# Products of 512 columns whose moving operand is read from its two halves in turn

## The chip, the core and the metric

The kernel runs on one core of a Trainium2 chip. The metric is the device time of one execution in microseconds (us), lower is better; the median of three runs stands for a kernel. The engines are named as in the profile: PE is TensorE with its matrix products, PEld its loads of stationary operands, DVE is VectorE, ACT ScalarE, POOL GpSimd, SP SyncE, whose queue issues most DMA transfers. Operands lie in SBUF, results of products in PSUM, in banks of 512 float32 columns on 128 partitions.

## What is computed

The reference is float32 throughout: two layers of a first block, then two layers of a second one, on 512 tokens of width 1024 (and, in the second, 256 tokens of context). Shortened to the products that matter:

```python
def swiglu(u, w_in, w_out):                     # w_in [1024, 2*2816], w_out [2816, 1024]
    gate, up = jnp.split(u @ w_in, 2, axis=-1)
    return (jax.nn.silu(gate) * up) @ w_out

# first block, layer l: FFN, mixer, FFN, each with residual, layer norm and modulation
f = swiglu(modulate(x, sh1, sc1), ffn_in[l, 0], ffn_out[l, 0])
x = deepnorm_residual(x, f, g1, ln_g[l, 0], ln_b[l, 0], 0.5)
u = modulate(x, sh2, sc2)
m = even_mixer(u, ...) if l % 2 == 0 else odd_mixer(u, ...)   # RG-LRU and linear attention / MLA
x = deepnorm_residual(x, m, g2, ln_g[l, 1], ln_b[l, 1])
f = swiglu(modulate(x, sh3, sc3), ffn_in[l, 1], ffn_out[l, 1])
x = deepnorm_residual(x, f, g3, ln_g[l, 2], ln_b[l, 2], 0.5)

# second block, layer l: one wide projection, three branches, their gated sum
h = rms_norm(x, norm_g[l]) * (1 + scale) + shift
(a_glu, a_gate, nq, nk, nv, n_gate, wq, wk, wv, w_gate, merge) = split(h @ w_in[l])  # [1024, 7936]
y = sig(g_a) * conv_branch(...) + sig(g_b) * neighbourhood(...) + sig(g_c) * window(...)
x = x + gate * (y @ w_o[l])
```

## The kernel before

[...] Each operand x is split into a part `hi`, rounded to float32r, and `lo = x - hi` (`split`, L118 on ACT and L119 on DVE; weights in `wsplit`, L129 and L130), and a product is hi·hi + hi·lo + lo·hi into one bank of PSUM. `mm3` (L148 to L153) writes this for a stationary weight block w of 128x128 and a moving operand x of up to 512 token columns:

```python
mm(out, lhsT=w[0], rhs=x[0], start=first, stop=False)   # L151
mm(out, lhsT=w[0], rhs=x[1], start=False, stop=False)   # L152
mm(out, lhsT=w[1], rhs=x[0], start=False, stop=last)    # L153
```

`lhsT` is the stationary operand, `rhs` the moving one. There are four families of products with 512 moving columns:

- Feature-major, `feat` and `ffn_first` through `mm3` (L151 to L153): the moving operand is the transposed activations `xTh`, `xTl` [128, 8, 512], eight k tiles for one bank. FFN inputs, the projections of the mixers and the MLA queries and keys are made so. With the first column pair of an FFN and a few others the tokens come in two slices of 256.
- Token-major, `tok_out.go` (L322, L323, L326): the outputs of FFNs and mixers. Stationary is a slice of 128 tokens of the activations (`gh`, `gl`), moving are 512 columns of the weights (`whi`, `wlo`), into eight banks for four token tiles and two halves of the 1024 columns.
- `proj_steps` (L1071, L1072, L1076): the wide projection of the second block, feature-major, and beside it products of 256 context columns (L1074, L1075, L1078).
- `out_proj.go` (L1851, L1852, L1855): the last projection of a layer of the second block, token-major.

Beside these stand products of 256 columns and fewer (attention scores, transposes, L1127 to L1129 token-major) and the plain float32 products of RG-LRU (L568).

What comes out of a bank is read by ACT or DVE: `gated` of the FFN by ACT (silu, L407) and DVE (product, L408), `resid_ln` by DVE (L285, then layer norm), the mixers by ACT (L613 to L716), the second block by ACT (L1605, L1649 to L1688, L1823) and DVE (L1616, L1618, L1651, L1653), the last result by DVE (L2299, followed by the output DMA).

The order of the work is that of the code: each engine has its own list, and units that follow one another by some ticks (`tick`, `push`) are emitted between products. Weights come through `raw` (L121), two buffers of 1 MB filled by SP's queue, and are split a unit ahead of their products. Modulation vectors for later layers are computed in the background (`bg_step`) on DVE from `gv` tiles.

Of the kernel before, what the change touches and what calls it, by code (L numbers as in the profile page):

```python
# [32 lines left out]

class Core:
# [98 lines left out]
    def wcols(self, w, c0, n=256, lows=None):  # L133
        """w [K, N] columns c0..c0+n as one unit; (hi, lo) [P, K/P, 128] per block."""
# [4 lines left out]
    def wrows(self, w, r0, a=2, gate=None, eng=None):  # L139
        """w [K, 1024] rows r0.. as one unit; (hi, lo) [P, 1, 1024] per k tile, columns times gate, on eng[j]."""  # L140
# [7 lines left out]
    def mm3(self, out, w, x, first, last):  # L148
        """out += w.T @ x, both in two parts; w stationary."""
# [20 lines left out]
    def rstd_fast(self, v, n, eps, scale):  # L170
        """the same, by a square root and a Newton step."""
# [26 lines left out]
    def load_cols(self, out, parts):  # L198
        """background steps: DRAM rows of 128 as the columns of out [P, rows]."""
# [6 lines left out]
    def gemv(self, w, accs):  # L206
        """accs: list of (acc tile [P, 1024], columns [P, 8]); one step per unit."""
# [17 lines left out]
    def col_fold(self, acc, tmp):  # L225
        """first half of the sum of acc [P, 1024 or 512] over the partitions; tmp like acc."""
# [6 lines left out]
    def col_fin(self, r, bcol, out):  # L233
        """second half, as columns, plus bcol."""
# [8 lines left out]
    def row_out(self, col, out):  # L243
        """columns [P, 8] to a row of DRAM."""
# [32 lines left out]
    def resid_ln(self, t, ps2):  # L277
        """x of token tile t, normalised."""
# [13 lines left out]
    def affine_rows(self, xs, g, b, scale, row, eng):  # L292
        """background steps: x*g*scale + b*scale for the tiles xs; g, b [1024] in DRAM, row: a tile for them."""
# [64 lines left out]
    def ffn_first(self, pool, g, w_in, weights, gated, first):  # L358
        """the first four column blocks of both parts; the operands come by halves of the k tiles,
# [2021 lines left out]
```

## Time and profile before

| | us |
|---|---|
| median of three runs (3640.43 to 3645.78) | 3644.38 |
| span of the profiled execution | 3646.3 |
| PE busy in it | 3522.6 |
| DVE busy | 2459.3 |
| ACT busy | 1446.6 |
| POOL busy | 654.7 |

A busy time is the time in which an engine has an instruction under way. Matrix products overlap in the records: one of 512 columns is shown as 0.39 to 0.40 us long, and the next begins 0.23 us after it. The distance between starts, or the length of a gapless window over its count of products, is thus what one costs. A line in the profile carries the line number of the code; a group "L151 PE MATMUL ps<-xTh,whi 128\*128 128x512" has the moving operand first, then the stationary one, the stationary shape, and the result's shape. A few per cent of the product records can be missing.

### The profile page before, as it was taken

To read this page: it belongs to the slowest core of one execution; us is meant where nothing else is said; L and a number is where in the kernel's file an instruction comes from. 1 tells how busy PE (TensorE), PEld (TensorE's weight loads), DVE (VectorE), ACT (ScalarE), POOL (GpSimd) and SP (SyncE) were. 2 spreads that over 40 slices of the span, in tenths; PEclk is the share of its full clock that TensorE was granted. 3 is DMA by queue.
4 is the path that set the end of the run, shared out by engine and by line. 5 is a ranking of instruction groups with operands and counts; after the bars stand their busy time and mean duration, and the time that the engine had idled before them with its cause. 6 is when DMAs were issued, how large, how long until landed. Compare 5 with 4: busy or idle time off the path is not lost. (4 is left out here: it accounts for less than half of the span.)

```text
span 3646.3 us, 49117 instructions
## 1 busy us (share of the span) xinstructions
PE 3522.6 (97%) x19303; PEld 2970.0 (81%) x19303; DVE 2459.3 (67%) x3978; ACT 1446.6 (40%) x2576; POOL 654.7 (18%) x734
## 2 busy tenths in 40 slices
PE   8999999999999999989999999989999999979999
PEld 6788887788878888878888898878888888868887
DVE  7665545866665785586886577797774467796854
ACT  3222344643223222364322265545323255546342
POOL 1200211000000000041000124696000133390001
PEclk9999999999999999999999999999999999999999
DMA  7762322236742663222663232211112243211233
GB/s 261 240 212 93 100 76 81 87 108 192 237 144 93 223 198 104 69 69 70 207 221 116 93 102 59 60 35 30 53 59 81 76 147 93 56 51 36 87 99 110
DMA packets 264739, 412.82 MB, mean 113 GB/s; under 512 B 16385, under 2 KB 209658, under 8 KB 264378
## 3 DMA queue, kind: packets, MB, share of 16 engines
q1 hardware_dynamic: 251274, 380.33, 32.1%
q0 software_dynamic: 9040, 23.31, 2.6%
q10 hardware_dynamic: 4192, 6.03, 0.5%
q8 instruction: 152, 2.49, 0.3%
q14 instruction: 81, 0.66, 0.1%
HBM read 395.45 MB, written 10.39 MB: 111 GB/s over the span
## 5 line engine op out<-in xcount | busy, mean ns | idle before, releaser
L129 ACT ACTIVATE whi<-raw 128x1024 fp32r<-128x1024 f32 (+2 forms) x532 | 538.2, 1015 | 1175.1 <-PE ps L152 470.1
L130 DVE TENSOR_TENSOR wlo<-raw,whi 128x1024 fp32r<-128x1024 f32 (+2 forms) x530 | 644.0, 1217 | 337.8 <-ACT whi L129 336.0
L151 PE MATMUL ps<-xTh,whi 128*128 128x512 f32 (+2 forms) x1971 | 737.5, 375 | 4.6 <-ACT xTh L118 3.7
L153 PE MATMUL ps<-xTh,wlo 128*128 128x512 f32 (+2 forms) x1971 | 726.7, 369 | 1.7 <-DVE wlo L130 1.6
L152 PE MATMUL ps<-xTl,whi 128*128 128x512 f32 (+2 forms) x1971 | 724.4, 368 | 2.3 <-DVE xTl L2091 1.6
L153 PEld LDWEIGHTS ps<-xTh,wlo 128*128 128x128 f32 (+1 forms) x1971 | 370.7, 188 | 70.3 <-DVE wlo L130 2.6
L151 PEld LDWEIGHTS ps<-xTh,whi 128*128 128x128 f32 (+1 forms) x1971 | 371.3, 188 | 68.3 <-ACT xTh L118 5.5
L152 PEld LDWEIGHTS ps<-xTl,whi 128*128 128x128 f32 (+1 forms) x1971 | 371.2, 188 | 67.1 <-DVE xTl L2091 2.4
L322 PE MATMUL ps<-whi,gh 128*128 128x512 f32 x872 | 346.6, 397 | 0.4 <-DVE g L408 0.4
L323 PE MATMUL ps<-wlo,gh 128*128 128x512 f32 x872 | 345.6, 396 | 0.0
L220 DVE SCALAR_TENSOR_TENSOR acc<-gv,cc,acc 128x1024 f32<-128x1024 f32 x189 | 240.3, 1282 | 148.6 <-DMA gv<-in_mod_w 115.5
L1071 PE MATMUL ps<-xTh,whi 128*128 128x512 f32 x704 | 284.9, 405 | 0.8 <-DVE oc L1292 0.8
L1076 PE MATMUL ps<-xTh,wlo 128*128 128x512 f32 x704 | 279.0, 396 | 0.0
L326 PE MATMUL ps<-whi,gl 128*128 128x512 f32 x872 | 274.6, 395 | 3.1 <-DVE gl L119 3.1
L1072 PE MATMUL ps<-xTl,whi 128*128 128x512 f32 x704 | 277.4, 394 | 0.0
L326 PEld LDWEIGHTS ps<-whi,gl 128*128 128x128 f32 x872 | 164.0, 188 | 44.1 <-DVE gl L119 4.0
L322 PEld LDWEIGHTS ps<-whi,gh 128*128 128x128 f32 x872 | 164.0, 188 | 40.5 <-DVE g L408 0.8
L323 PEld LDWEIGHTS ps<-wlo,gh 128*128 128x128 f32 x872 | 164.1, 188 | 38.5
L118 ACT ACTIVATE gh<-g 128x512 fp32r<-128x512 f32 x88 | 55.6, 632 | 307.4 <-PE ps L323 272.0
L119 DVE TENSOR_TENSOR gl<-g,gh 128x512 fp32r<-128x512 f32 x88 | 60.8, 691 | 149.6 <-ACT gh L118 149.6
L1071 PEld LDWEIGHTS ps<-xTh,whi 128*128 128x128 f32 x704 | 133.6, 190 | 29.4 <-DVE oc L1292 1.1
L166 POOL TENSOR_SCALAR rs_y<-mv 128x1 f32<-128x1 f32 x24 | 8.9, 370 | 777.8 <-DVE mv L287 750.9
(741 smaller groups left out, 7090.7 us busy)
## 6 DMA issues: line engine op xcount, KB each, us to landing
raw<-in_ffn_in SPq DMA_DIRECT2D x88, 1024.0 KB
gv<-in_mod_w SPq DMA_DIRECT2D x128, 512.0 KB
raw<-in_w_in SPq DMA_DIRECT2D x62, 1024.0 KB
raw<-in_ffn_out SPq DMA_DIRECT2D x44, 1024.0 KB
gv<-in_w_ada SPq DMA_DIRECT2D x48, 512.0 KB
raw<-in_even_w_in SPq DMA_DIRECT2D x20, 1024.0 KB
raw<-in_w_o SPq DMA_DIRECT2D x12, 1024.0 KB
raw<-in_even_w_out SPq DMA_DIRECT2D x8, 1024.0 KB
```

The source lines that it names most:

```text
L129: self.w_last = self.nc.scalar.activation(hi, view, AF.Copy).ins
L130: (low or self.nc.vector).tensor_tensor(lo, view, hi.bitcast(F32), op=ALU.subtract)
L151: mm(out, lhsT=w[0], rhs=x[0], start=first, stop=False)
L152: mm(out, lhsT=w[0], rhs=x[1], start=False, stop=False)
L153: mm(out, lhsT=w[1], rhs=x[0], start=False, stop=last)
L220: nc.vector.scalar_tensor_tensor(acc, r, cc[:, k:k + 1], acc, op0=ALU.mult, op1=ALU.add)
L322: mm(ps[t][h], lhsT=a[0][:, sl], rhs=b[0][:, 0, hs], start=f, stop=False)
L323: mm(ps[t][h], lhsT=a[0][:, sl], rhs=b[1][:, 0, hs], start=False, stop=False)
L326: mm(ps[t][h], lhsT=a[1][:, sl], rhs=b[0][:, 0, hs], start=False, stop=l)
L1071: mm(px, lhsT=wh[:, k, :], rhs=xh[:, k, :], start=f, stop=False)
L1072: mm(px, lhsT=wh[:, k, :], rhs=xl[:, k, :], start=False, stop=False)
L1076: mm(px, lhsT=wl[:, k, :], rhs=xh[:, k, :], start=False, stop=l)
```

## The change

Three views are added. `il` puts the columns of a moving operand in the order 0, 256, 1, 257, ..., 255, 511: for each n first column n of the left half, then column n of the right. `un` reads a bank that was written in that order so that the columns come in the old order: all even columns, then all odd ones, a step of two float32. `hv` gives any other operand of the same instruction the same two-level shape and leaves its order as it is.

```diff
+def il(x):
+    return x.rearrange("p (a n) -> p n a", a=2)
+def un(ps):
+    return ps.rearrange("p (n a) -> p a n", a=2)
+def hv(x):
+    return x.rearrange("p (a n) -> p a n", a=2)
...
     def feat(self, out, wb, xh, xl, sl):
         kt = wb[0].shape[1]
+        v = il if sl.stop - sl.start == S else lambda x: x
         for k in range(kt):
-            self.mm3(out, (wb[0][:, k, :], wb[1][:, k, :]), (xh[:, k, sl], xl[:, k, sl]),
+            self.mm3(out, (wb[0][:, k, :], wb[1][:, k, :]), (v(xh[:, k, sl]), v(xl[:, k, sl])),
...
     def resid_ln(self, t, ps2):
-            nc.vector.tensor_tensor(x[:, sl], x[:, sl], ps2[h], op=ALU.add)
+            nc.vector.tensor_tensor(hv(x[:, sl]), hv(x[:, sl]), un(ps2[h]), op=ALU.add)
...
     def tok_out(...), in go:
-                mm(ps[t][h], lhsT=a[0][:, sl], rhs=b[0][:, 0, hs], start=f, stop=False)
-                mm(ps[t][h], lhsT=a[0][:, sl], rhs=b[1][:, 0, hs], start=False, stop=False)
+                mm(ps[t][h], lhsT=a[0][:, sl], rhs=il(b[0][:, 0, hs]), start=f, stop=False)
+                mm(ps[t][h], lhsT=a[0][:, sl], rhs=il(b[1][:, 0, hs]), start=False, stop=False)
...
-                mm(ps[t][h], lhsT=a[1][:, sl], rhs=b[0][:, 0, hs], start=False, stop=l)
+                mm(ps[t][h], lhsT=a[1][:, sl], rhs=il(b[0][:, 0, hs]), start=False, stop=l)
...
     in ffn_first:
-                        self.mm3(p[j], w[j][k], (self.xTh[:, k, :], self.xTl[:, k, :]), k == 0, k == KT - 1)
+                        self.mm3(p[j], w[j][k], (il(self.xTh[:, k, :]), il(self.xTl[:, k, :])), k == 0, k == KT - 1)
...
     in ffn:
-            def gated(jp, ps):
+            def gated(jp, ps, v=un):
                 for j in range(2):
-                    s = g[:, jp * 2 + j, :]
-                    nc.scalar.activation(s, ps[0][j], AF.Silu)
-                    nc.vector.tensor_tensor(s, s, ps[1][j], op=ALU.mult)
+                    s = hv(g[:, jp * 2 + j, :])
+                    nc.scalar.activation(s, v(ps[0][j]), AF.Silu)
+                    nc.vector.tensor_tensor(s, s, v(ps[1][j]), op=ALU.mult)
...
     in proj_steps (L1071, L1072, L1076; out_proj.go alike):
-                    mm(px, lhsT=wh[:, k, :], rhs=xh[:, k, :], start=f, stop=False)
-                    mm(px, lhsT=wh[:, k, :], rhs=xl[:, k, :], start=False, stop=False)
+                    mm(px, lhsT=wh[:, k, :], rhs=il(xh[:, k, :]), start=f, stop=False)
+                    mm(px, lhsT=wh[:, k, :], rhs=il(xl[:, k, :]), start=False, stop=False)
...
     in the last layer's result (L2299):
-                    nc.vector.tensor_tensor(xw[:, sl], xw[:, sl], ps[h], op=ALU.add)
+                    nc.vector.tensor_tensor(hv(xw[:, sl]), hv(xw[:, sl]), un(ps[h]), op=ALU.add)
```

All other instructions that read a bank of these products get `un` and `hv` in the same way: L613, L629 (second head pair only), L636, L702, L716, the splits of the MLA queries and keys, L1384, L1605, L1616, L1618, L1649, L1651, L1653, L1679, L1688 and L1823. Where the tokens come in two slices of 256 the products stay in the plain order, and the reading instruction takes `hv` in place of `un`. Products of 256 columns, the scores of MLA and all plain float32 products are as before. Comments and docstrings are removed too, so that line numbers shift.

## Rows read from the trace of the kernel before

**Rows 1.** The page: PE's busy time, and the granted clock in slices
```profile
PE 3522.6 (97%) x19303; PEld 2970.0 (81%) x19303; DVE 2459.3 (67%) x3978; ACT 1446.6 (40%) x2576; POOL 654.7 (18%) x734
...
PEclk9999999999999999999999999999999999999999
```

**Rows 2.** Windows: us, busy PE PEld DVE ACT POOL, clock, DMA share, GB/s
```profile
300.00:390.00 90.00, 90.00 (x387) 72.41 (x386) 46.49 (x46) 25.29 (x32) 0.59 (x1) 1.00 0.30 101
...
1200.00:1260.00 60.00, 60.00 (x264) 49.24 (x263) 47.31 (x58) 17.21 (x23) 0.00 (x0) 1.00 0.68 224
...
3380.00:3630.00 250.00, 250.00 (x1074) 202.15 (x1073) 155.75 (x198) 86.90 (x117) 17.35 (x7) 1.00 0.32 101
```

**Rows 3.** Timeline of PE at 1205 and 3400 us: start us, length us, line
```profile
1204.99 0.39 PE L151 MATMUL ps<-xTh,whi 128*128 128x512 f32 x1
...
1206.60 0.39 PE L152 MATMUL ps<-xTl,whi 128*128 128x512 f32 x1
...
3399.82 0.40 PE L1076 MATMUL ps<-oh,wlo 128*128 128x512 f32 x1
...
3402.87 0.40 PE L1071 MATMUL ps<-oh,whi 128*128 128x512 f32 x1
```

**Rows 4.** Timeline of PE at 630 us (plain float32) and 2150 us (256 columns)
```profile
629.73 1.02 PE L568 MATMUL ps<-xc,rg_wa 128*128 128x512 f32 x2
...
632.31 1.02 PE L568 MATMUL ps<-xc,rg_wx 128*128 128x512 f32 x2
...
2149.76 0.28 PE L1127 MATMUL ps<-whi,xTh 128*128 128x256 f32 x1
...
2151.91 0.28 PE L1128 MATMUL ps<-wlo,xTh 128*128 128x256 f32 x1
```

**Rows 5.** PE by line: xcount | busy us, mean ns | idle before <-releaser
```profile
L151 PE MATMUL ps<-xTh,whi 128*128 128x512 f32 x1541 | 614.5, 399 | 0.8 <-ACT xTh L2089 0.8
...
L322 PE MATMUL ps<-whi,gh 128*128 128x512 f32 x872 | 346.6, 397 | 0.4 <-DVE g L408 0.4
...
L1071 PE MATMUL ps<-xTh,whi 128*128 128x512 f32 x704 | 284.9, 405 | 0.8 <-DVE oc L1292 0.8
...
L326 PE MATMUL ps<-whi,gl 128*128 128x512 f32 x872 | 274.6, 395 | 3.1 <-DVE gl L119 3.1
...
L1851 PE MATMUL ps<-whi,gh 128*128 128x512 f32 x128 | 51.4, 407 | 0.0
```

**Rows 6.** DVE by line and form, columns as in group 5
```profile
L408 DVE TENSOR_TENSOR g<-g,ps 128x512 f32<-128x512 f32 x88 | 59.9, 681 | 50.4 <-PE ps L153 50.0
...
L1618 DVE TENSOR_TENSOR sg<-sg,ps 128x512 f32<-128x512 f32 x32 | 21.8, 680 | 37.8 <-PE ps L1076 31.1 <-ACT whi L129 6.7
...
L1252 DVE TENSOR_TENSOR ps<-ps,bm 128x256 f32<-128x256 f32 x32 | 19.1, 616 | 4.3 <-PE ps L1228 4.3
...
L1252 DVE TENSOR_TENSOR ps<-ps,bm 128x192 f32<-128x192 f32 x32 | 15.1, 496 | 14.8 <-PE ps L1228 14.8
...
L1618 DVE TENSOR_TENSOR sg<-sg,ps 128x256 f32<-128x256 f32 x16 | 6.6, 414 | 0.0
```

**Rows 7.** ACT by line and form, columns as in group 5
```profile
L407 ACT ACTIVATE g<-ps 128x512 f32<-128x512 f32 x88 | 51.0, 580 | 0.1
...
L1384 ACT ACTIVATE vT<-ps 128x512 f32<-128x512 f32 x8 | 9.7, 1215 | 0.2
```

**Rows 8.** Timeline of the end of the span, columns as in group 3
```profile
3640.66 0.40 PE L1855 MATMUL ps<-whi,gl 128*128 128x512 f32 x1
...
3641.09 0.69 DVE L2299 TENSOR_TENSOR xw<-xw,ps 128x512 f32<-128x512 f32 x1 [2.11 <-PE ps L1855]
```

**Rows 9.** Windows at the start, columns as in group 2
```profile
0.00:100.00 100.00, 84.77 (x359) 70.45 (x360) 71.67 (x104) 36.50 (x50) 13.65 (x16) 0.95 0.76 253
...
100.00:200.00 100.00, 98.07 (x430) 79.20 (x429) 67.79 (x95) 25.83 (x31) 22.71 (x42) 1.00 0.79 254
...
120.00:124.00 4.00, 4.00 (x20) 3.26 (x19) 3.97 (x6) 0.07 (x1) 0.00 (x0) 1.00 0.96 321
```

More of the change, by code (lines that the diff above doesn't have):

```diff
@@ L421, in ffn @@
                             self.pop_tail()
-                gated(jp, pss)
+                gated(jp, pss, un if jp else hv)
             def act(k):
@@ L612, in out_gate @@
                         self.feat(ps, gb[j], xh, xl, full)
-                        nc.scalar.activation(dst[:, j, :], ps, AF.Silu)
+                        nc.scalar.activation(hv(dst[:, j, :]), un(ps), AF.Silu)
                         self.tick()
@@ L628, in even @@
                         for j in range(2):
-                            nc.scalar.activation(qk[i][:, j, :], pss[i][j], AF.Copy)
+                            nc.scalar.activation(hv(qk[i][:, j, :]), (un if hp else hv)(pss[i][j]), AF.Copy)
                     if hp == 0:
@@ L635, in even @@
                         self.feat(psz[:16, :], wz, xh, xl, full)
-                        nc.vector.tensor_copy(zb, psz[:16, :])
+                        nc.vector.tensor_copy(hv(zb), un(psz[:16, :]))
                     for h2 in range(2):
@@ L701, in even @@
                         nc.gpsimd.memset(xp[:, 0:3], 0.0)
-                        nc.scalar.activation(xp[:, 3:3 + S], ps, AF.Copy)
+                        nc.scalar.activation(hv(xp[:, 3:3 + S]), un(ps), AF.Copy)
                         xps.append(xp)
@@ L985, in qk_of @@
                         ps = self.pst()[:, :sl.stop - sl.start]
+                        wide = sl.stop - sl.start == S
+                        v, back, to = (il, un, hv) if wide else (lambda x: x,) * 3
                         for k, wk in enumerate(ws_):
-                            self.mm3(ps, wk, (x_[0][:, k, sl], x_[1][:, k, sl]), k == 0, k == len(ws_) - 1)
-                        self.split(ps, d[0][:, sl], d[1][:, sl])
+                            self.mm3(ps, wk, (v(x_[0][:, k, sl]), v(x_[1][:, k, sl])), k == 0, k == len(ws_) - 1)
+                        self.split(back(ps), to(d[0][:, sl]), to(d[1][:, sl]))
                 def v_new():
@@ L1075, in proj_steps @@
                         mm(pc, lhsT=wh[:, k, :], rhs=cl[:, k, :], start=False, stop=False)
-                    mm(px, lhsT=wl[:, k, :], rhs=xh[:, k, :], start=False, stop=l)
+                    mm(px, lhsT=wl[:, k, :], rhs=il(xh[:, k, :]), start=False, stop=l)
                     if both:
@@ L1604, in emit_g @@
                     sg = gp.tile([P, NTOK], F32, tag="sg", name=self.nm("sg"), bufs=2)
-                    nc.scalar.activation(sg[:, :S], px, AF.Sigmoid)
+                    nc.scalar.activation(hv(sg[:, :S]), un(px), AF.Sigmoid)
                     if both:
@@ L1611, in emit_y @@
                     sg, y, last = gates[j], yT[:, n0 + j, :], None
-                    for p, sl in ((px, slice(0, S)), (pc, slice(S, NTOK))):
+                    for p, sl, v in ((px, slice(0, S), un), (pc, slice(S, NTOK), hv)):
                         if p is None:
@@ L1615, in emit_y @@
                         if first:
-                            last = nc.vector.tensor_tensor(y[:, sl], sg[:, sl], p, op=ALU.mult).ins
+                            last = nc.vector.tensor_tensor(hv(y[:, sl]), hv(sg[:, sl]), v(p), op=ALU.mult).ins
                         else:
-                            nc.vector.tensor_tensor(sg[:, sl], sg[:, sl], p, op=ALU.mult)
+                            nc.vector.tensor_tensor(hv(sg[:, sl]), hv(sg[:, sl]), v(p), op=ALU.mult)
                             nc.vector.tensor_tensor(y[:, sl], y[:, sl], sg[:, sl], op=ALU.add)
@@ L1644, in emit @@
         def emit(j, px, pc):
-            for p, sl in ((px, slice(0, S)), (pc, slice(S, NTOK))):
+            for p, sl, v in ((px, slice(0, S), un), (pc, slice(S, NTOK), hv)):
                 if p is None:
@@ L1648, in emit @@
                 sg = gp.tile([P, width], F32, tag="p", name=self.nm("sgate"), bufs=4)[:, :p.shape[1]]
-                nc.scalar.activation(sg, p, AF.Tanh, scale=0.5)
+                nc.scalar.activation(hv(sg), v(p), AF.Tanh, scale=0.5)
                 if g == 0:
-                    nc.vector.scalar_tensor_tensor(oT[:, 2 + j, sl], sg, 1.0, p, op0=ALU.add, op1=ALU.mult)
+                    nc.vector.scalar_tensor_tensor(hv(oT[:, 2 + j, sl]), hv(sg), 1.0, v(p), op0=ALU.add, op1=ALU.mult)
                 else:
-                    nc.vector.scalar_tensor_tensor(sg, sg, 1.0, p, op0=ALU.add, op1=ALU.mult)
+                    nc.vector.scalar_tensor_tensor(hv(sg), hv(sg), 1.0, v(p), op0=ALU.add, op1=ALU.mult)
                     nc.vector.tensor_tensor(oT[:, j, sl], oT[:, j, sl], sg, op=ALU.mult)
@@ L1676, in conv_in, with emit_lin, emit_sig @@
         cT = [x[:, :NTOK] for x in [pool.tile([P, NTOK], F32, name=self.nm("conv"))] + blocks[:3]]
-        def emit_lin(j, px, pc):
-            nc.scalar.activation(blocks[j][:, PAD:PAD + S], px, AF.Copy)
+        def emit_lin(j, px, pc, v=un):
+            nc.scalar.activation(hv(blocks[j][:, PAD:PAD + S]), v(px), AF.Copy)
             if both:
                 nc.scalar.activation(blocks[j][:, W + PAD:W + PAD + CTX], pc, AF.Copy)
-        def emit_sig(j, px, pc, sp=pool, tag="sg", width=512, bufs=1):
-            for p, o, n in ((px, PAD, S), (pc, W + PAD, CTX)):
+        def emit_sig(j, px, pc, sp=pool, tag="sg", width=512, bufs=1, v=un):
+            for p, o, n, v in ((px, PAD, S, v), (pc, W + PAD, CTX, hv)):
                 if p is None:
@@ L1687, in emit_sig @@
                 sg = sp.tile([P, width], F32, tag=tag, name=self.nm("sg"), bufs=bufs)
-                nc.scalar.activation(sg[:, :n], p, AF.Sigmoid)
+                nc.scalar.activation(hv(sg[:, :n]), v(p), AF.Sigmoid)
                 b = blocks[j][:, o:o + n]
@@ L1714, in conv_in @@
         for j in range(2):
-            emit_lin(j, pxs[0][j], pcs[0][j])
+            emit_lin(j, pxs[0][j], pcs[0][j], hv)
         for j in range(2):
-            emit_sig(j, pxs[1][j], pcs[1][j])
+            emit_sig(j, pxs[1][j], pcs[1][j], v=hv)
         def rest(i, sp, width):
@@ L1817, in emit @@
         def emit(j, px, pc):
-            for p, sl in ((px, slice(0, S)), (pc, slice(S, NTOK))):
+            for p, sl, v in ((px, slice(0, S), un), (pc, slice(S, NTOK), hv)):
                 if p is None:
@@ L1850, in go @@
                 hs = slice(h * 512, (h + 1) * 512)
-                mm(ps[t][h], lhsT=a[0][:, sl], rhs=b[0][:, 0, hs], start=f, stop=False)
-                mm(ps[t][h], lhsT=a[0][:, sl], rhs=b[1][:, 0, hs], start=False, stop=False)
+                mm(ps[t][h], lhsT=a[0][:, sl], rhs=il(b[0][:, 0, hs]), start=f, stop=False)
+                mm(ps[t][h], lhsT=a[0][:, sl], rhs=il(b[1][:, 0, hs]), start=False, stop=False)
             for h in halves:
                 hs = slice(h * 512, (h + 1) * 512)
-                mm(ps[t][h], lhsT=a[1][:, sl], rhs=b[0][:, 0, hs], start=False, stop=l)
+                mm(ps[t][h], lhsT=a[1][:, sl], rhs=il(b[0][:, 0, hs]), start=False, stop=l)
         for k0 in range(0, KT, 2):
```

6 lines of the change are left out of this document (3 added, 3 removed).

## The prediction

> **What bounds the kernel now.** I read the page's busy times first: TensorE (PE) is busy 3522.6 of 3646.3 us, 97%, VectorE (DVE) 67%, ScalarE (ACT) 40%, and the clock row stands at 9, its highest digit, in every slice [rows 1]. So 3646.3 − 3522.6 = 124 us at most is waiting; the rest is the rate at which products pass. That rate is what the change touches, so next come the windows in which PE runs nothing but products of 512 columns. [...] A record's own 0.39 to 0.40 us is of no use here, since records overlap; the distance between starts is. In the timeline the feature-major products start (1206.60 − 1204.99)/7 = 230 ns apart, those of the last layer (3402.87 − 3399.82)/13 = 235 ns [rows 3]. By the counts of the built program 4,695 products of L151 to L153 at some 229 ns and 5,856 others at some 232.6 ns give a mean of 231.0 ns.
>
> [...]
>
> **The change, part by part.** The views come first. Of 18,461 products in the built program 10,551 read their moving operand in the order 0, 256, 1, 257, ... These are the products of [rows 5], of which the trace misses a few per cent; 72 products of 512 columns in MLA keep the plain order, as do all of 256 columns and less. All five engines hold the same instructions in the same order as before, and the products write PSUM in one run as before. So nothing moves, and what changes is (a) the price of a column at the array, (b) the price of a result read out of PSUM at a step of two, (c) waits.
>
> (a) No row shows a moving operand read in two places in turn. The nearest rows are on DVE: a stride of 32 elements on one operand raises a column from (680 − 414)/256 = 1.04 ns (L1618) to (616 − 496)/64 = 1.88 ns (L1252) [rows 6]. [...] If fetches in two places overlap, the feed is no longer the limit and the price falls to the array's. [...] I take 216.5 ns, 1.5 ns above L568's quarter, since some rest of the feed is more likely than none: **10,551 × (231.0 − 216.5) = −153 us.**
>
> [...]
>
> (b) 212 ACT and 229 DVE instructions of 512 columns now read PSUM at a step of two: L407 at 580 ns, L408 and L1618 at 681 and 680 ns, are the commonest [rows 6, 7]. Below: nothing, if a step of eight bytes in PSUM is as good as four. Above: the hop of L1252, (616 − 414)/256 = 0.79 ns a column against L1618, so 0.40 us more each on DVE, and on ACT that of L1384, which writes SBUF at a stride, 1215 − 580 = 635 ns [rows 6, 7]. In all that would be 229 × 0.40 = 92 us on DVE and 212 × 0.635 = 135 us on ACT, at shares of 67% and 40%. What hides them is that the next pair of banks is being filled meanwhile: PE's own rows give 0.4 us of idle time before 872 products for L408 and 3.1 us for the split behind it [rows 5], while DVE idles 50.4 us in front of L408 and 37.8 us in front of L1618, for PE above all [rows 6]. Bare they are only where a stage ends: 8 ends (four FFNs, two mixers, two layers) with the two halves of the last tile, 8 × 2 × 0.40 = 6 us, and the last gated blocks of four FFNs, 4 × (0.64 + 0.40) = 4 us. One such end is the very last tile, where L2299 begins 0.43 us after the last product's start [rows 8]. Between 0 and 10 us I take **+5 us**.
>
> (c) Three added waits stand on POOL, 37 on PE; those on PE are on products of PE itself, 13 or more places back, at least 3 us earlier. They cost nothing; without that distance each would cost one product's pipeline, about 0.16 us (0.39 − 0.23), 6 us for all.
>
> **What comes late next.** Weights and modulation rows are loaded in the background. From 300 us on the DMA share is 0.30 to 0.68 in streams without a gap [rows 2]; products shorter by 231/216.5 make 0.73 of it. In the first 200 us it is 0.76 and 0.79, and 0.96 in one stretch [rows 9]; there loads may set the pace. The 789 products of these 200 us would gain at most 789 × 14.5 ns = 11 us; I count half as lost: **+5 us.** DVE would be at 2459 + 92 of 3500 us, 73% at worst, and doesn't become the bound.
>
> **Sum.** 3646.3 − 153 + 5 + 5 = 3503 us of span. The span of the profiled execution lies 1.9 us above the median of 3644.38 us, so 3501 us, rounded to **3500 us**.
>
> **Rivals.**
> 1. The number of pieces, or of columns, sets the feed's rate, and their order doesn't matter. [...] Against it: streams of the same shape differ by 5 ns with their operands [rows 2], so the place of the data counts. It gives 3644 to 3655 us (0 to 10 us from (b)).
> 2. A slower kernel: every change of place costs a fetch, since only one piece is held at a time. For it speak L1252 and L1384, where a stride costs 1.8 times the contiguous price or more. Against it, these strides never come back to the piece they left, and the new order does so after one column. The mechanism sits in all 10,551 products, and it decides as soon as a change of place costs over 14.5/512 = 0.03 ns. At DVE's ratio, 1.88/1.04 = 1.8, a product is 416 ns: 10,551 × 185 ns = +1.95 ms, 5.6 ms in all; at 1.88 ns a column it is 960 ns, +7.7 ms, 11.3 ms. [...]
> 3. PSUM reading is the price: a step of two costs as in the upper bounds and lies bare oftener than I think, with the banks coming free late. With no gain at the array and a quarter of the 92 + 135 us bare this is 3700 us; with the gain, 3555 us, which is inside the likeliest case.
> 4. The change doesn't do what it says: the compiler could straighten the two-part view. The built access patterns hold it on all 10,551 products, so I give it nothing of its own; it would look like rival 1.
>
> **How the numbers follow.** About 0.2% (7 us) is what a measurement of this kernel can tell from no change. The forecast, the feed freed wholly or in part, has 0.68: 3475 (231 to 215 ns, 10,551 × 16 = 169 us) to 3600 us (a third of the gain kept, or most of (b) bare). Rival 1 has 0.14, of which 0.13 within 0.2% and 0.01 slower. Rival 2 has 0.13 and rival 3, with products no faster, 0.05; both are slower. So faster 0.68, same 0.13, slower 0.19. The likeliest case's own range is 3475 to 3600 us. For 8 in 10 rival 1 is taken in with its (b), up to 3665 us; left out is rival 2 and most of rival 3.
>
> **What would show it.** Right: in the windows of pure 512-column streams the length over the count falls to some 216 ns at a clock of 1.00, in all three families by about the same end price, hence by more in the token-major and the last-layer products than in L151 to L153; products of 256 columns and L568 keep 113 and 860 ns; L407, L408 and L285 within 0 to 0.64 us of their old durations; PE's share falls by a point or two, since its gaps stay. Wrong: prices of 227 to 233 ns as before (rival 1), or 400 ns and more (rival 2); or shorter products with new idle time on PE behind DVE or ACT (rival 3) or behind DMA in the first 200 us. A price between 217 and 227 ns would mean that the feed has a second limit which I don't see.

## The result, and the profile after

The changed kernel takes 3550.01 us (median; 3545.52 to 3560.9) beside 3645.08 us for the kernel before in the same comparison: a ratio of 0.9736, 95% interval 0.9713 to 0.9759. Of the six executions of a kernel told of below, that with a third buffer, one passed at a lower granted clock (0.752, 4309.60 us), and its median is of the other five. The span of the profiled execution is 3551.0 us, 95.3 us less than before. The page:

```profile
PE 3388.9 (95%) x19303; PEld 2995.1 (84%) x19303; DVE 2457.3 (69%) x3978; ACT 1442.3 (41%) x2576; POOL 651.6 (18%) x734
...
PEclk9999999999999999999999999999999999989999
DMA  7763322236743663212664232211122243211233
```

PE is busy 133.7 us less than in [rows 1] (3522.6 to 3388.9), but the span is only 95.3 us shorter: PE's idle time went from 123.7 to 3551.0 − 3388.9 = 162.1 us. The price of a product is again read from windows without a gap (columns as in [rows 2]), here a stretch of an FFN, a feature-major one, and the last layer, and from the distance of starts in the timeline (columns as in [rows 3]):

```profile
1390.00:1490.00 100.00, 100.00 (x465) 87.58 (x464) 54.32 (x57) 27.90 (x35) 0.75 (x2) 1.00 0.27 88
1176.00:1237.00 61.00, 56.99 (x266) 49.59 (x264) 45.77 (x60) 17.67 (x23) 0.00 (x0) 1.00 0.72 244
3304.00:3518.00 214.00, 213.45 (x989) 186.51 (x989) 151.32 (x193) 84.82 (x115) 16.06 (x7) 1.00 0.35 113
```

```profile
1204.76 0.38 PE L166 MATMUL ps<-xTh,whi 128*128 128x512 f32 x1
...
1206.28 0.38 PE L167 MATMUL ps<-xTl,whi 128*128 128x512 f32 x1
```

100.00/465 = 215.1 ns, and in the last layer 213.45 busy us over 989 = 215.8 ns; in the feature-major stretch starts lie (1206.28 − 1204.76)/7 = 217 ns apart. All families have come to the same price, at a granted clock of 1.00 as before, when [rows 2] gave 90.00/387 = 232.6 ns token-major, 60.00/264 = 227.3 ns feature-major and 250.00/1074 = 232.8 ns in the last layer. The count of a window takes in products that only reach over its ends (of the 465, 463 start inside), so a quotient of this kind is up to 2 ns low here and in [rows 2]; the distance of starts is the better measure. Over all records of 512 float32r columns that follow within 300 ns (10,326 in either trace) the mean distance fell from 231.0 to 216.9 ns. Products that keep the plain order kept their price: 113 to 114 ns at 256 columns of the first mixer (L651 to L653, now L667 to L669; (2151.91 − 2149.76)/19 = 113.2 ns for those in [rows 4]), and for L568, now L584, 860 ns for a pair of records ((632.31 − 629.73)/3 in [rows 4]).

Results read out of PSUM at a step of two cost what they cost before. These are the groups of DVE and ACT that answer to L408, L285, L1618, L407 and L1384 [rows 6, 7]:

```profile
L424 DVE TENSOR_TENSOR g<-g,ps 128x512 f32<-128x512 f32 x88 | 60.0, 681 | 34.3 <-PE ps L168 33.8
...
L301 DVE TENSOR_TENSOR xs<-xs,ps 128x512 f32<-128x512 f32 x48 | 31.1, 681 | 18.2 <-PE ps L342 18.2
...
L1636 DVE TENSOR_TENSOR sg<-sg,ps 128x512 f32<-128x512 f32 x32 | 21.8, 682 | 32.6 <-PE ps L1094 32.5
```

```profile
L423 ACT ACTIVATE g<-ps 128x512 f32<-128x512 f32 x88 | 51.0, 581 | 0.1
...
L1402 ACT ACTIVATE vT<-ps 128x512 f32<-128x512 f32 x8 | 9.2, 1151 | 0.2
```

L424 stays at 681 ns, 680 becomes 682 and 580 becomes 581 ns; L1402, whose read-out also changed its order of writing, went from 1215 to 1151 ns.

What PE waited for has grown. The view of waits of PE (total us, times, longest), first of before, then of after; L166 to L168 are the old L151 to L153, L342 is L326, L263 is L247:

```profile
PE ps L151 <- ACT xTh L118: 3.7, 4, 1.1
...
PE ps L326 <- DVE gl L119: 3.1, 2, 2.7
...
PE ps L247 <- DVE rowc L2026: 2.7, 1, 2.7
...
PE ps L153 <- DVE wlo L130: 1.6, 1, 1.6
```

```profile
PE ps L168 <- DVE wlo L145: 14.6, 5, 5.8
PE ps L263 <- DVE rowc L2044: 14.1, 5, 5.5
...
PE ps L166 <- ACT xTh L133: 6.4, 5, 1.8
PE ps L342 <- DVE gl L134: 6.3, 2, 5.8
...
PE ps L211 <- DMA vt<-in_cln_b: 3.8, 1, 3.8
```

The waits for `wlo` grew by 13.0 us, for `rowc` by 11.4, for `gl` by 3.2, for `xTh` by 2.7. One of the stalls in full: DVE's timeline ahead of the weight split that the products wait for, and PE's timeline behind it.

```profile
993.89 2.60 DVE L236 SCALAR_TENSOR_TENSOR acc<-gv,cc,acc 128x1024 f32<-128x1024 f32 x2 [1.37 <-DMA gv<-in_mod_w]
996.41 1.22 DVE L145 TENSOR_TENSOR wlo<-raw,whi 128x1024 fp32r<-128x1024 f32 x1
998.77 1.28 DVE L236 SCALAR_TENSOR_TENSOR acc<-gv,cc,acc 128x1024 f32<-128x1024 f32 x1 [1.14 <-DMA gv<-in_mod_w]
1000.09 1.25 DVE L244 STREAM_TRANSPOSE gv<-acc 128x1024 f32<-128x1024 f32 x1
1001.37 0.69 DVE L424 TENSOR_TENSOR g<-g,ps 128x512 f32<-128x512 f32 x1
1001.97 1.21 DVE L246 TENSOR_REDUCE cf<-gv 128x32 f32<-128x1024 f32 x1
1003.10 1.21 DVE L145 TENSOR_TENSOR wlo<-raw,whi 128x1024 fp32r<-128x1024 f32 x1
```

```profile
1004.37 0.80 PE L168 MATMUL ps<-xTh,wlo 128*128 128x512 f32 x1 [5.82 <-DVE wlo L145]
1004.96 0.63 PE L166 MATMUL ps<-xTh,whi 128*128 128x512 f32 x1
...
1008.80 0.63 PE L166 MATMUL ps<-xTh,whi 128*128 128x512 f32 x1
...
1009.54 0.38 PE L168 MATMUL ps<-xTh,wlo 128*128 128x512 f32 x1
1009.76 0.38 PE L166 MATMUL ps<-xTh,whi 128*128 128x512 f32 x1
```

```profile
1000.00:1009.00 9.00, 4.63 (x11) 3.72 (x12) 8.94 (x10) 2.60 (x3) 0.00 (x0) 0.64 0.24 94
```

DVE works off the background sums (L236), and behind them the fold of the vector (L244, L246) and the FFN's L424, before it comes to the split `wlo` at 1003.10 us. At 998.77 a sum has waited 1.14 us for its load, which stands in the list ahead of the split. PE has nothing to do for 5.82 us. Then it starts slowly: from 1004.96 to 1008.80 us nine products pass at 427 ns each, at half the granted clock (0.50 in these 3.84 us, 0.64 in the window), before the distance is 215 ns again. Of such products at 415 to 445 ns, called cold below, there are 69 in the trace of before and 128 in that of after, and the mean granted clock went from 0.990 to 0.984.

### The profile page after: what moved, and what is told of

It reads as the page before. It is cut to its first block, busy times and chain, and to the rows that moved or that the text cites. A ratio compares the mean times of both kernels' runs of the same rounds, so it can differ in the third digit from the quotient of the medians.

```text
span 3551.0 us, 49157 instructions
## 1 busy us (share of the span) xinstructions
PE 3388.9 (95%) x19303; PEld 2995.1 (84%) x19303; DVE 2457.3 (69%) x3978; ACT 1442.3 (41%) x2576; POOL 651.6 (18%) x734
## 5 line engine op out<-in xcount | busy, mean ns | idle before, releaser
L166 PE MATMUL ps<-xTh,whi 128*128 128x512 f32 (+2 forms) x1971 | 719.9, 366 | 7.3 <-ACT xTh L133 6.4
L168 PE MATMUL ps<-xTh,wlo 128*128 128x512 f32 (+2 forms) x1971 | 711.8, 361 | 14.6 <-DVE wlo L145 14.6
L167 PE MATMUL ps<-xTl,whi 128*128 128x512 f32 (+2 forms) x1971 | 711.3, 361 | 2.3 <-DVE xTl L2109 1.6
L168 PEld LDWEIGHTS ps<-xTh,wlo 128*128 128x128 f32 (+1 forms) x1971 | 374.7, 190 | 60.5 <-DVE wlo L145 16.9
L166 PEld LDWEIGHTS ps<-xTh,whi 128*128 128x128 f32 (+1 forms) x1971 | 375.4, 191 | 53.7 <-ACT xTh L133 8.5
L236 DVE SCALAR_TENSOR_TENSOR acc<-gv,cc,acc 128x1024 f32<-128x1024 f32 x189 | 240.4, 1283 | 156.7 <-DMA gv<-in_mod_w 117.8
L338 PE MATMUL ps<-whi,gh 128*128 128x512 f32 x872 | 332.9, 382 | 0.5 <-DVE g L424 0.5
L339 PE MATMUL ps<-wlo,gh 128*128 128x512 f32 x872 | 331.7, 380 | 0.0
L1089 PE MATMUL ps<-xTh,whi 128*128 128x512 f32 x704 | 276.6, 393 | 0.0
L1094 PE MATMUL ps<-xTh,wlo 128*128 128x512 f32 x704 | 270.6, 384 | 0.0
L1090 PE MATMUL ps<-xTl,whi 128*128 128x512 f32 x704 | 269.7, 383 | 0.0
L342 PE MATMUL ps<-whi,gl 128*128 128x512 f32 x872 | 261.0, 381 | 6.3 <-DVE gl L134 6.3
L342 PEld LDWEIGHTS ps<-whi,gl 128*128 128x128 f32 x872 | 165.4, 190 | 30.6 <-DVE gl L134 7.1
L160 DVE TENSOR_TENSOR raw<-raw,gr 128x1024 f32<-128x1024 f32 x104 | 123.0, 1221 | 32.7 <-DMA raw<-in_ffn_out 27.5
```

The source lines that it names most:

```text
L236: nc.vector.scalar_tensor_tensor(acc, r, cc[:, k:k + 1], acc, op0=ALU.mult, op1=ALU.add)
L338: mm(ps[t][h], lhsT=a[0][:, sl], rhs=il(b[0][:, 0, hs]), start=f, stop=False)
L339: mm(ps[t][h], lhsT=a[0][:, sl], rhs=il(b[1][:, 0, hs]), start=False, stop=False)
L342: mm(ps[t][h], lhsT=a[1][:, sl], rhs=il(b[0][:, 0, hs]), start=False, stop=l)
L1089: mm(px, lhsT=wh[:, k, :], rhs=il(xh[:, k, :]), start=f, stop=False)
L1090: mm(px, lhsT=wh[:, k, :], rhs=il(xl[:, k, :]), start=False, stop=False)
```

## Experiments on the order of the columns

My theory going in read the price of before as that of the feed of the moving operand: a fetch from one place lasts some 1.8 ns, and fetches from two places overlap. It was an estimate: one column at DVE's stride of 32 takes (616 − 496)/64 = 1.88 ns [rows 6], and at 229 ns a product PE takes four columns in 1.79 ns; no row showed a fetch of PE. Seven kernels, each run once, read the moving operand in other orders, with the same instructions otherwise. By a piece I mean four neighbouring columns, 16 bytes. The diff is that of the one function (`un` and `hv` follow where named):

```diff
 def il(x):
-    return x.rearrange("p (a n) -> p n a", a=2)        # the changed kernel: 0, 256, 1, 257
+    return x.rearrange("p (a n i) -> p n a i", a=2, i=2)   # e1_pairs:    0, 1, 256, 257, 2, 3
+    return x.rearrange("p (b a i) -> p b i a", a=2, i=4)   # e2_near:     0, 4, 1, 5, 2, 6, 3, 7, 8, 12
+    return x.rearrange("p (n a) -> p a n", a=2)            # e3_evenodd:  0, 2, 4, ..., 1, 3 (un, hv follow)
+    return x.rearrange("p (n a) -> p a n", a=4)            # e4_stride4:  0, 4, 8, ..., 1, 5 (un, hv follow)
+    return x.rearrange("p (a n) -> p n a", a=4)            # e5_quarters: 0, 128, 256, 384, 1 (un, hv follow)
+    return x.rearrange("p (b a i) -> p b i a", a=2, i=2)   # e6_swap:     0, 2, 1, 3, 4, 6, 5, 7
+    return x.rearrange("p (a n i) -> p n a i", a=2, i=4)   # e9_quads:    0, 1, 2, 3, 256, 257, 258, 259
```

Below each expectation stand the time and one row of windows, from a stretch of the same FFN in which PE has products of 512 columns only. For comparison, the kernel before in that stretch, 100.00/430 = 232.6 ns:

```profile
1430.00:1530.00 100.00, 100.00 (x430) 80.47 (x429) 49.51 (x51) 26.26 (x33) 0.00 (x0) 1.00 0.26 88
```

**Pairs.** 

> The 10,551 products read their halves in turn two columns at a time (0, 1, 256, 257, 2, 3, ...); results are read out at the same step of two as in the changed kernel, so that columns end up in another order (the values are then not the reference's, the work is the same). Overlap theory (two pieces of 16 bytes are open at once, and the fetch of one hides behind the reading of the other): a piece is left after two columns and met again two columns later, still two pieces are open, 216 ns a product, 3550 us as the changed kernel. Rival, single columns matter (it is the change of place at every column that helps): the price goes half way back, some 223 ns, 10,551 x 7 = 74 us more, about 3620 us.

4643.23 us, and 150.00/446 = 336 ns a product. Both forecasts missed by far: taking two neighbours in a row from each half is not half as good as one, it is much worse than the plain order.

```profile
1930.00:2080.00 150.00, 150.00 (x446) 87.10 (x445) 52.35 (x55) 29.90 (x35) 0.75 (x2) 1.00 0.18 59
```

**Near pieces.** 

> The products alternate between two neighbouring pieces of 16 bytes (0, 4, 1, 5, 2, 6, 3, 7, then 8, 12, ...) and not between the halves; results are read out in the changed kernel's way, so columns end up in another order. Overlap theory: two pieces are open here too, but both are asked for within one column and then both are used up after eight, so the pair has to be fetched as fast as in the plain order; if what counts is only that two fetches overlap, 216 ns and 3550 us. Rival, the place counts (the two halves, 1 KB apart, lie in parts of SBUF that can be read side by side, neighbouring pieces do not): at least the old 231 ns, 3645 us, or more, up to 1.8 ns for each change of place that is not covered, 416 ns and 5.6 ms.

3553.2 us, 215.1 ns. Where single columns alternate, the distance is without weight: two neighbouring pieces do as well as two halves, 215.1 ns in either. The rival that the place counts falls.

```profile
1390.00:1490.00 100.00, 100.00 (x465) 87.63 (x465) 54.32 (x57) 27.76 (x35) 0.75 (x2) 1.00 0.27 88
```

**Even and odd columns.** 

> The products read all even columns, then all odd ones: a step of 8 bytes, every 16-byte piece is met by two columns in a row and then again half a product later; results are read out in the order that puts this right. One place at a time, 256 fetches in place of 128. Overlap theory with a fetch of 1.8 ns from one place: 256 x 1.8 = 460 ns a product, 10,551 x (460 - 216) = 2.57 ms more than the changed kernel, 6.1 ms. Rival, two hits on a piece are enough at PE's rate (fetches are pipelined, and not their number is the limit): 216 to 231 ns, 3550 to 3650 us.

5890.56 us, 220.00/486 = 453 ns. Near the 460 ns of my theory, but the next run shows that this was for another reason.

```profile
2520.00:2740.00 220.00, 220.00 (x486) 101.33 (x485) 55.98 (x56) 32.24 (x38) 0.00 (x0) 1.00 0.14 45
```

**Every fourth column.** 

> The products read every fourth column, four times over: each column in another piece of 16 bytes than the one before, and none met again before 128 columns have passed, 512 fetches; results are read out in the order that puts this right. Overlap theory with 1.8 ns for a fetch from one place: 512 x 1.8 = 920 ns a product, 10,551 x 704 = 7.4 ms more than the changed kernel, 11.0 ms. Rival, a change of place costs PE nothing at all and the excess before came from something else in the plain order: 216 ns, 3550 us.

5972.86 us, 220.00/479 = 459 ns. With twice as many changes of piece as in the run before the price is the same within 1.5%. A fetch of 1.8 ns from one place, on which my step (a) rested, doesn't exist on PE: 459/512 = 0.90 ns a column, half of it.

```profile
2560.00:2780.00 220.00, 220.00 (x479) 99.41 (x478) 54.76 (x56) 30.70 (x36) 0.00 (x0) 1.00 0.13 45
```

Here I gave up the theory and formed another, from the prices so far (215, 215, 233, 336, 453 and 459 ns): PE takes the columns at even and at odd positions by two separate paths, and each path is the faster the more of its own successive columns lie in one 16-byte piece. In the plain order a path gets two (0, 2, then 4, 6), in the changed order four (0, 1, 2, 3), in the two runs above one.

**Quarters.** 

> The products read four quarters in turn (0, 128, 256, 384, 1, 129, ...), results are read out at a step of four, which puts the order right. Theory of two alternating readers (formed after the runs with pairs, near pieces, even and odd columns, every fourth column: PE takes the columns at even and at odd positions by two paths, each of which is fast while its own columns stay in one piece of 16 bytes): the even path sees 0, 256, 1, 257, ..., a change of piece at every access as in the run with pairs, so at least its 327 ns, up to the 460 ns of every fourth column: 1,270 us beside the products + 10,551 x 0.327 to 0.460 = 4.7 to 6.1 ms. Rival, several pieces are simply held open (four as well as two): 216 ns, 3550 us.

4083.02 us, 140.00/503 = 278 ns. Several open pieces as such don't help (that would be 216 ns): the order of four places is worse than the plain one, as the theory of two paths wants it, but the size was misjudged; an order in which each path comes back to its piece three more times costs less than the 327 ns that I had taken for the pairs.

```profile
1640.00:1780.00 140.00, 140.00 (x503) 95.51 (x502) 58.65 (x62) 29.66 (x36) 0.75 (x2) 1.00 0.22 70
```

**Swap inside a piece.** 

> The products read 0, 2, 1, 3, 4, 6, 5, 7, ...: alternation inside one 16-byte piece; results are read out in the changed kernel's way, so columns end up in another order. Theory of two alternating readers, form one (each path wants neighbouring columns in a row): the even path sees 0, 1, 4, 5, the odd one 2, 3, 6, 7, so half of the changed order's good neighbours are there; form two (the excess of the plain order comes from both paths in the same piece at once): both still share each piece, so the price stays at the old 229 to 233 ns or rises, 3645 us or more. If form one alone is at work, 216 ns and 3550 us. Rival, distance or halves: excluded by the run with near pieces, nothing expected of it.

3650.12 us beside 3646.1 us for the kernel before, 232.6 ns, the plain price to the digit. Neighbouring columns for a path are not the point (form one falls); two columns of a piece for each path give the plain price here too, in another order. Form two, that the excess comes from both paths being in the same piece at once, forecast this price as well and is not excluded.

```profile
1430.00:1530.00 100.00, 100.00 (x430) 80.47 (x429) 50.24 (x50) 27.84 (x35) 0.00 (x0) 1.00 0.25 83
```

**Runs of four.** 

> The products take four columns of one half, then four of the other (0, 1, 2, 3, 256, 257, 258, 259, 4, ...); results are read out in the changed kernel's way, so columns end up in another order. Theory of two alternating readers (columns at even and at odd positions are fetched by two paths, each of which is at full rate when it takes a whole piece of four columns in a row): here each path takes two columns of a piece and then two of another, as in the plain order, so the price is about the plain one, 227 to 238 ns, 3645 us, or a little above. Rival, what helps is a longer time between neighbouring pieces or the two halves as such: 216 ns, 3550 us.

3833.53 us, 120.00/470 = 255 ns. The rival at 216 ns falls: alternating halves doesn't help when a path gets two columns of a piece at a time. The theory's number, 227 to 238 ns, was too low by some 20 ns; leaving for the other half after two columns costs something that the plain order, whose next piece is the neighbour, doesn't pay (255 ns against 233). Here the place does count, and why is open.

```profile
1510.00:1630.00 120.00, 120.00 (x470) 88.68 (x469) 53.89 (x54) 29.79 (x36) 0.00 (x0) 1.00 0.25 82
```

All orders in one table, with what the supposed path of the even positions would see:

| order | even positions | of one piece in a row | both paths in one piece | ns a product |
|---|---|---|---|---|
| halves (changed kernel) | 0, 1, 2, 3 | 4 | no | 215 |
| near pieces | 0, 1, 2, 3, 8 | 4 | no | 215 |
| plain (before) | 0, 2, 4, 6 | 2 | yes | 233 |
| swap | 0, 1, 4, 5 | 2 | yes | 233 |
| runs of four | 0, 2, 256, 258 | 2, then the other half | yes | 255 |
| quarters | 0, 256, 1, 257 | 1, piece met three more times at once | no | 278 |
| pairs | 0, 256, 2, 258 | 1, piece met once more at once | yes | 336 |
| even and odd | 0, 4, 8 | 1 | yes | 453 |
| every fourth | 0, 8, 16 | 1 | no | 459 |

Sorted by the columns of a piece that a path takes in a row, and then by how often the piece is met again at once, the nine orders stand in their sequence; no other reading that I have does this. The second key was added after the times were known. That there are two paths, and that 16 bytes are their unit, is inferred from these times and not seen; the prices between 233 and 453 ns are not derived from it, and neither are the 22 ns between the plain order and the runs of four.

One rival stands untested. In every order with two columns in a row both paths share a piece, and in both fast orders they don't, so the step from 233 to 215 ns may come from the longer run or from the separate pieces. Every fourth column beside even and odd columns says that separate pieces alone gain nothing at one column in a row (459 and 453 ns). An order such as 0, 8, 1, 9, 4, 12, 5, 13, with two in a row and separate pieces, would tell; it was not run.

That the price lies in the order of reading, and is no fixed extra cost of a product, is borne out by stretches at half the granted clock. Products in pairs, 336 ns at a granted clock of 1.00, start (4106.88 − 4103.46)/8 = 428 ns apart in one (granted clock 0.50 from 4101 to 4107 us):

```profile
4103.46 0.63 PE L1090 MATMUL ps<-xTl,whi 128*128 128x512 f32 x1
...
4106.88 0.63 PE L1089 MATMUL ps<-xTh,whi 128*128 128x512 f32 x1
```

This is what products of the plain order and of the halves cost there, 427 ns as the median of the cold ones in either trace; the 18 ns between these two at a granted clock of 1.00 are gone, which a fixed extra cost of each product would not be. Every fourth column, 459 ns at 1.00, keeps its price: (36.66 − 33.88)/6 = 463 ns (granted clock 0.51 from 33.4 to 36.9 us).

```profile
33.88 0.65 PE L166 MATMUL ps<-xTh,whi 128*128 128x512 f32 x1
...
36.66 0.65 PE L166 MATMUL ps<-xTh,whi 128*128 128x512 f32 x1
```

So I read these runs as two rates, of which the slower sets the price: one goes with the granted clock (215 ns at 1.00 and 427 ns at 0.50 with the halves), the other is that of the feed in the order at hand, which half the clock did not slow (459 and 463 ns at every fourth column).

## Experiments on the time that was missing

The products gave 146 us and the span fell by 95. The theory: what is missing lies on DVE's queue in the FFN's input stretches, where background sums wait for loads ahead of weight splits, and in the cold products behind each stall.

Two runs cut the background vectors to half, in the kernel before and in the changed one:

```diff
-            self.nc.sync.dma_start(out=r, in_=w[k * P:(k + 1) * P, :])
-            self.gemv_step(r, k, accs)
+            h = slice(0, 512)
+            self.nc.sync.dma_start(out=r[:, h], in_=w[k * P:(k + 1) * P, h])
+            if k == 0:
+                for acc, _ in accs:
+                    self.nc.vector.memset(acc[:, 512:], 0.0)
+            self.gemv_step(r[:, h], k, [(acc[:, h], cc) for acc, cc in accs])
```

> The kernel before, with the background vectors cut: each modulation row's product with the matrix loads and sums only the first 512 of 1024 columns (half of the loads of these matrices and half of their VectorE time left out; the other half of the vectors is zero). Theory that the missing 50 us went into waits on VectorE's queue, where the sums stand ahead of the weight splits and wait for their loads: the kernel before has little of these waits (1.6 us for wlo, 2.7 us for rowc), so it gains under 15 us: 3630 to 3645 us. Rival, the sums were slowing it too: below 3620 us.

> The changed kernel with the same cut (first 512 of 1024 columns of the background vectors). Theory of the waits on VectorE's queue: the waits for wlo (14.6 us), rowc (14.1 us) and their cold products go, and the distance to the cut kernel before grows from 95 us to about 130 to 150 us: 3490 to 3510 us. Rival, the gain is lost elsewhere (evacuation, attention stages, the clock on its own): the distance stays at 95 to 105 us, 3530 to 3550 us.

3637.69 us (0.9973 of before, 0.9961 to 0.9986) and 3526.61 us (0.9663, 0.9641 to 0.9684). The distance is 111.1 us, against 3646.1 − 3550.0 = 96.1 us: 15 us of the missing 50 come back, uncertain by some 12 us by the three intervals. The traces bear the size out: PE's idle time is 113.1 us in the cut kernel before and 141.2 us in the cut changed one, 28.1 us more instead of 38.4, and cold products are 80 and 111, 31 more instead of 59. That is between the two forecasts, and PE's waits in the cut changed kernel say why:

```profile
PE ps L267 <- DVE rowc L2048: 10.6, 3, 5.9
...
PE ps L168 <- DVE wlo L145: 1.5, 1, 1.5
```

The waits for `wlo` are gone (14.6 to 1.5 us), those for `rowc` are not (14.1 to 10.6 us). The fold of the vector (L244, L246 and their like) is not cut by this edit, and PE's transposes behind it wait for the chain on DVE.

The next run leaves all work in place and gives the loads a third buffer:

```diff
-            r = self.gv.tile([P, D], F32, tag="gv", name=self.nm("gv"), bufs=2)
+            r = self.gv.tile([P, D], F32, tag="gv", name=self.nm("gv"), bufs=3)
...
-                h = pool.tile([P, S], F32R, tag="gh", name=self.nm("gh"), bufs=5)
+                h = pool.tile([P, S], F32R, tag="gh", name=self.nm("gh"), bufs=4)
```

> The changed kernel with three buffers in place of two for the rows of the modulation matrices (and, to make room in SBUF, four in place of five for the FFN's split activations). Theory: of the new stalls some come from background sums that wait for their loads on VectorE's queue ahead of weight splits (155 us of such waits in all); with a third buffer the loads are there earlier, the 14.6 us before the products on wlo fall below 5 us, and the kernel gains 10 to 25 us: 3525 to 3540 us. Rival, the loads are bound by the DMA engines, not by the buffers, or the fourth buffer of the activations is missed: no gain, 3545 us or more.

3523.30 us (0.9651 of before, 0.9634 to 0.9669): 27 us below the changed kernel, and the fastest with all work in place. DVE's waits for the loads of the sums, in the changed kernel and here, and this kernel's busy times:

```profile
DVE acc L236 <- DMA gv<-in_mod_w: 117.8, 76, 4.2
DVE acc L236 <- DMA gv<-in_w_ada: 37.7, 26, 3.8
```

```profile
DVE acc L236 <- DMA gv<-in_mod_w: 63.7, 41, 5.2
...
DVE acc L236 <- DMA gv<-in_w_ada: 4.8, 6, 1.2
```

```profile
PE 3379.1 (96%) x19303; PEld 2991.4 (85%) x19303; DVE 2456.2 (70%) x3978; ACT 1442.8 (41%) x2576; POOL 649.7 (18%) x734
```

The sums' waits fell from 155.5 to 68.5 us, the waits of L168 for `wlo` left the list, those for `rowc` fell from 14.1 to 6.3 us, and cold products went from 128 to 79. PE's idle time is 3521.5 − 3379.1 = 142.4 us, 20 us less than in the changed kernel; 19 us more than in the kernel before stay. So the two buffers, more than the DMA engines, held the loads back. How much the third buffer would have given the kernel before was not tried, so how much of the gain is time that the change had lost is not shown; the half cut gave the kernel before 8 us.

Another possible cause, PE's transposes that come too soon behind DVE's fold, was tried by distance:

```diff
     in cols_job and rows_job, between the last sum and PE's fold or transpose:
-            for _ in range(3):
+            for _ in range(6):
                 yield
```

> The changed kernel with six in place of three background steps between the last sum of a modulation vector and the PE instructions that fold and transpose it. Theory: these PE instructions stand in PE's list at a distance in products from the VectorE work that they wait for; shorter products have shortened that distance in time, whence 14.1 us of waits for rowc against 2.7 us before. [...] Rival, VectorE is late as a whole in these stretches, and the wait only moves to the next weight split: 3545 us or more.

The theory wanted the waits for `rowc` below 4 us, the cold products behind them gone too, and 3530 to 3540 us. The kernel took 3560.57 us (0.9756, 0.9738 to 0.9774): no gain, rather a loss; the intervals of the two kernels overlap. The waits for `rowc` fell to 0.2 us, PE's idle time stayed (162.1 and 161.6 us), and the waits for the weight splits grew from 14.6 us to

```profile
PE ps L168 <- DVE wlo L145: 23.9, 10, 6.0
```

So the rival was right: DVE is late as a whole in these stretches, and which PE instruction finds it late is a matter of order. With all work left in place, only taking DVE's own waits away (the third buffer) helped.

The last run adds the halves for the feature-major products of 256 columns to the six steps:

```diff
     def feat(self, out, wb, xh, xl, sl):
-        v = il if sl.stop - sl.start == S else lambda x: x
+        v = il
...
+def un2(ps):                                  # two slices of 256 in one bank
+    return ps.rearrange("p (s n a) -> p s a n", s=2, a=2)
...
     in proj_steps:
-                        mm(pc, lhsT=wh[:, k, :], rhs=ch[:, k, :], start=f, stop=False)
+                        mm(pc, lhsT=wh[:, k, :], rhs=il(ch[:, k, :]), start=f, stop=False)
```

> As the run with six steps, and the feature-major products with 256 moving columns (context columns of the wide projection, the slices of 256 tokens) also read their two halves in turn, some 2,700 products, results put right at read-out. Theory of two alternating readers: these products fall from 117 to 120 ns to 108 to 110 ns, 2,700 x 9 = 24 us at most, some of it taken back by waits: 10 to 20 us below the run with six steps. Rival, at 256 columns the excess is no matter of the feed but of the change between products: no gain over the run with six steps.

3543.88 us (0.9712, 0.9695 to 0.9729), 16.7 us below the run with six steps alone, intervals apart. The products of FFN slices of 256 columns, in the changed kernel and here:

```profile
407.89 0.28 PE L166 MATMUL ps<-xTh,whi 128*128 128x256 f32 x1
...
410.72 0.28 PE L166 MATMUL ps<-xTh,whi 128*128 128x256 f32 x1
```

```profile
409.66 0.28 PE L181 MATMUL ps<-xTh,whi 128*128 128x256 f32 x1
...
410.67 0.28 PE L181 MATMUL ps<-xTh,whi 128*128 128x256 f32 x1
```

24 products in 2.83 us are 118 ns before, 9 in 1.01 us are 112 ns here: 6 ns where I had expected 9; the context products of the wide projection (L1074, now L1092 and L1107) went from 119 to 109 ns. So reading the halves in turn gains at 256 columns too. This edit together with the third buffer was not run; each alone gained.

## Why the prediction came out as it did

The forecast was 3500 us, the likeliest case's range 3475 to 3600, and the result is 3550.01: faster, as forecast, with 95 us of the 144 us. By its steps:

| term | forecast, us | measured, us |
|---|---|---|
| (a) products | −153 | −146 (10,326 × 14.1 ns) |
| (b) reading PSUM at a step of two | +5 | 0 (681, 682, 581 ns) |
| (c) added waits | 0 | 0 seen |
| late loads and all other waiting of PE | +5 | +38.4 (idle time 123.7 to 162.1) |
| products at 427 ns behind stalls | not counted | +12.4 (59 more × 211 ns) |
| sum | −143 | −95 (the span: −95.3) |

The 10,326 are the products whose distance could be taken; with all 10,551 the first term is −149 us, so the sum closes to some 3 us only.

**(a) was right in size and wrong in its reason.** 216.5 ns forecast, 215 to 217 found, in all families, as said. But no run shows what the 216.5 ns came from: a floor of 215 ns taken as a quarter of L568's 860 ns [rows 4], and a fetch of 1.8 ns for each place, read off DVE's strided rows [rows 6]; what the runs show in its place is 215.1 ns with the halves and with near pieces. The runs with every second and every fourth column (453 and 459 ns, some 0.9 ns a column) show that PE has no such price, those with near pieces and runs of four that neither the distance of the two pieces nor a longer time between neighbouring pieces makes the gain. By my reason pairs would have been as good, and they cost 336 ns: that the order chosen was a fast one was luck. The floor of 215 ns held, as none of the nine orders came below it; why a quarter of L568 should be that floor was not shown.

**(b) was safe at its lower end.** The upper bound from L1252 and L1384 [rows 6, 7] was a stride in SBUF over 32 and 8 elements; a step of two in PSUM is no such thing (681 ns before and after in the FFN's product on DVE).

**The step that failed is "what comes late next".** I looked for it in shares: DVE at 73% at worst, DMA at 0.73. Both averages were right (DVE 69%, DMA 0.72 in the feature-major stretch above) and answer the wrong question. In the FFN's input stretches DVE's list had hardly a break even before: from 1200 to 1260 us it was busy for 47.3 us [rows 2] and waited 11.6 us for loads of background sums. That list has the weight split behind the sum that waits. Products that pass 6% sooner meet that split before it is done. The page of the kernel before shows these waits, 148.6 us of idle time in front of the sums, nearly all behind loads:

```profile
L220 DVE SCALAR_TENSOR_TENSOR acc<-gv,cc,acc 128x1024 f32<-128x1024 f32 x189 | 240.3, 1282 | 148.6 <-DMA gv<-in_mod_w 115.5
```

I gave this term 5 us in the first 200 us, where it was about right (803 products instead of 789 pass there, worth 3 of the 11 us, so some 8 were lost), and nothing after. The sign that I had named for being wrong, shorter products with new idle time of PE behind DVE, is in the trace.

**The clock was not in the sum.** The longer stalls at L168, L211, L263 and L342, 2.6 to 5.8 us, are followed by five to eleven products at 427 ns; over the whole span this adds about a third to the price of the waiting (12.4 beside 38.4 us). The rows of before had this too (0.95 in the first 100 us [rows 9]).

Rival 1 is excluded by the price of 215 ns, rival 2 by the same, though it lies close by: in other orders, in the runs with pairs, even and odd, and every fourth column, the loss is there, 336 to 459 ns. Rival 3 named the right kind of loss, stalls of PE behind other engines, at the wrong place; PSUM had no part in it.

## What to carry to other kernels

Where a stream of float32r products of 512 columns costs some 233 ns each at a granted clock of 1.00, as here, read the moving operand so that the columns at even and at odd positions each stay in a 16-byte piece of their own for four in a row (halves or neighbouring pieces in turn, 215 ns here), and undo the order at the read-out, where a step of two was free here (681 ns before and after); other orders cost up to twice the plain price (459 ns), so measure the spacing of starts. Before you count a gain of a few per cent on the engine that sets the pace, look in the fast stretches for instructions of other engines that wait for loads ahead of what this engine needs: an engine's mean share hides them, and a third buffer for the loads gained 27 us here.

## What the runs showed of the chip that I had not expected

- Two columns taken together from each of two places cost 336 ns a product where single columns cost 215 ns and the plain order, neighbours all through, 233 ns.
- Strided reading costs PE the same at two strides: 453 ns at every second, 459 ns at every fourth column, 0.9 ns a column against 1.88 ns on DVE [rows 6]. At half the granted clock every fourth column still costs 463 ns, while the pairs go from 336 to 428 ns.
- After a stall of 5.82 us some ten products passed at 427 ns each, at a granted clock of 0.50; such products were 69 before and 128 after, though the mean granted clock hardly shows it (0.990 and 0.984).
